# A hybrid decoder step: the next block's output projection before both halves of the last down part

## The chip, the cores and the metric

The kernel runs as one program on one core of one Trainium2 chip. The metric is the device time of an execution in microseconds (us); lower is better. The engines work side by side and wait for each other by semaphores: TensorE (PE, matmuls and transposes), VectorE (DVE), ScalarE (ACT), GpSimd (POOL), and SyncE (SP), which here issues nearly all DMAs in one fixed order.

## What is computed

One inference step of one decoder layer, for a prompt of 2048 tokens and a sample of 8 sequences of 8 tokens (64 rows). Cut to what matters here:

```
mix = concat(retention, stick_breaking_attention) @ w_out      # 1024 -> 1024
x   = x + g_m * mix
h   = rmsnorm(x, norm_ffn) * (1 + sc_f) + sh_f
a, bval = h @ w_up_gate, h @ w_up_val                           # 1024 -> 2816 each
conv = conv_b + sum_j a_ext[:, j:j+t] * conv_w[j]               # causal, width 3
ff  = (silu(conv) * bval) @ w_down                              # 2816 -> 1024
y   = rmsnorm(x + g_f * ff, norm_final)
```

Every matmul of these lines is done as three: each operand is split into a high and a low part of 32 bits each, and the products high x high, high x low and low x high are summed (`mm3`, lines 310 to 312).

## The kernel before, in words

The prompt is cut into four blocks of 512 tokens, each of four tiles of 128 tokens; the sample's 64 rows ride along with the last block as a fifth tile. After the input projections come two streams that are woven into one program: `attention([1, 2, 3])` and `mlps()` (line 1576). `mlps` does, block after block, the output projection with its residual and norm (`out_block`, line 1247) and the MLP (`ffn_block`, line 1327). Both are generators; `_weave` always steps the one that is behind by its share of planned work. The instructions that come out are then ordered on each engine by the framework's scheduler, so the order of the code is a guide and not the last word.

`ffn_block` goes over the 22 column tiles of the hidden layer in four parts of 6, 6, 6 and 4 (`PARTS`). A part does its up projections (features on the partitions, `act` is the moving operand), then its down projection in two halves of 512 output columns, each into four PSUM banks `d` (the sample's into a bank `z`), and adds them to the residual rows `x2` (`residual`, line 1321: DVE multiplies the bank by the gate `gp` into `hf`, then DVE or POOL adds `hf` to the rows `ff`). There are only four `d` banks, so a half can begin on a bank when `residual` of the half before has read it.

In the last part, the next block's `out_block` is run between the two halves (line 1422, `got = yield from after`). `out_block` loads two gates, the eight mixed-feature tiles `act<-mx` (512 KB each, into the same two `act` tiles that the up projection has just read), the four rows of `x`, and `w_out` in four loads of 1 MB (`raw`, two buffers). ACT and DVE split each `raw` in two pairs `whl` (three pairs fit). It returns a generator of features: normalised rows (`c`, `a`), PE transposes them (L416), ACT and DVE scale, shift and split them into `act` for the next up projection. In the second half, which goes tile by tile, one step of it is run after each tile; before the half, one step is run as well.

## Time and profile before

| | us |
|---|---|
| median of 3 runs | 3330.89 (3329.63 to 3334.44) |
| the profiled execution, its own time | 3337.49 |
| its span in the trace | 3335.8 |
| PE busy in the span | 3201.6 (96%) |
| DVE / ACT / POOL busy | 2086.6 / 1580.0 / 1023.7 |

The profiled execution is 6.6 us above the median. Matmuls are pipelined and their busy times overlap, so the pace of PE is read from one start to the next, and its idle time from the gaps that the timeline shows. The clock in a view is the granted clock of TensorE as a share of its full 2.4 GHz, averaged over the stretch; it has two levels, full and half.

### The profile page before, as it was taken

Reading aid. Unit: us, or ns where it says so; the run is one execution under the profiler, and the core shown is the slowest. Engines: PE = TensorE matmul, PEld = TensorE weight load, DVE = VectorE, ACT = ScalarE, POOL = GpSimd, SP = SyncE. Lnnn points to the kernel's source line nnn. Section 1 sums busy time; section 2 is a strip of 40 time slices with the busy share of each in tenths; the row PEclk is TensorE's granted clock in tenths of the full one; section 3 lists DMA queues with packets and bytes.
Section 4 is the critical chain, followed back from the end, with each engine's and each line's share of the span. In section 5 each row is a group of like instructions: output and inputs, shape, how many; then the busy total and the mean of one; then the engine's idle time right before and its main releaser. Section 6 shows DMA issues by size and latency. Waiting matters only on the chain. (4 is left out here: it accounts for less than half of the span.)

```text
span 3335.8 us, 50095 instructions
## 1 busy us (share of the span) xinstructions
PE 3201.6 (96%) x17879; PEld 2601.1 (78%) x17879; DVE 2086.6 (63%) x2989; ACT 1580.0 (47%) x2796; POOL 1023.7 (31%) x1841
## 2 busy tenths in 40 slices
PE   7999999999999889999999999999999999999998
PEld 5886777666887778878877778877788787799997
DVE  3245344245766587777778787787887873644445
ACT  3345335234444365555556455556555543533323
POOL 2012012013432343433444334344442432312113
PEclk8999999999999999999999999999999999999999
DMA  7757877885667843343454334354433335232221
GB/s 251 248 177 228 275 260 250 275 277 177 189 189 226 252 127 115 113 133 108 133 186 133 105 117 119 107 169 137 129 111 107 118 98 177 93 101 71 95 77 68
DMA packets 404247, 526.99 MB, mean 158 GB/s; under 512 B 25974, under 2 KB 242153, under 8 KB 403998
## 3 DMA queue, kind: packets, MB, share of 16 engines
q1 hardware_dynamic: 370078, 472.27, 45.3%
q10 hardware_dynamic: 33920, 51.52, 4.2%
q8 instruction: 142, 2.33, 0.3%
q14 instruction: 107, 0.88, 0.1%
HBM read 442.11 MB, written 81.60 MB: 157 GB/s over the span
## 5 line engine op out<-in xcount | busy, mean ns | idle before, releaser
L183 ACT CAST whl<-raw 128x1024 fp32r<-128x1024 f32 x408 | 427.5, 1049 | 1091.3 <-PE d L311 798.4
L165 DVE TENSOR_TENSOR whl<-raw,whl 128x1024 fp32r<-128x1024 f32 x408 | 517.8, 1270 | 577.0 <-ACT whl L183 568.8
L310 PE MATMUL d<-act,whl 128*128 128x512 f32 (+2 forms) x2016 | 745.0, 370 | 4.3 <-ACT whl L183 2.3
L312 PE MATMUL d<-act,whl 128*128 128x512 f32 (+2 forms) x2016 | 735.9, 365 | 1.2 <-DVE whl L165 1.2
L311 PE MATMUL d<-act,whl 128*128 128x512 f32 (+2 forms) x2016 | 733.7, 364 | 3.3 <-DVE act L165 2.4
L310 PEld LDWEIGHTS d<-act,whl 128*128 128x128 f32 x2016 | 384.8, 191 | 73.4 <-issue 11.1
L312 PEld LDWEIGHTS d<-act,whl 128*128 128x128 f32 x2016 | 383.9, 190 | 61.1 <-DVE whl L165 2.2
L311 PEld LDWEIGHTS d<-act,whl 128*128 128x128 f32 x2016 | 385.7, 191 | 58.7 <-DVE act L165 2.6
L310 PE MATMUL d<-whl,ff 128*128 128x512 f32 x704 | 279.3, 397 | 0.0
L311 PE MATMUL d<-whl,ff 128*128 128x512 f32 x704 | 278.8, 396 | 0.0
L312 PE MATMUL d<-whl,ff 128*128 128x512 f32 x704 | 278.1, 395 | 0.0
L310 PE MATMUL d<-whl,act 128*128 128x512 f32 x640 | 260.8, 409 | 10.3 <-ACT whl L183 9.2
L312 PE MATMUL d<-whl,act 128*128 128x512 f32 x640 | 258.5, 404 | 0.0
L311 PE MATMUL d<-whl,act 128*128 128x512 f32 x640 | 258.3, 404 | 0.0
L1172 DVE TENSOR_TENSOR_SCAN aom<-aom,acy 128x512 f32<-128x512 f32 x192 | 256.0, 1333 | 2.4 <-ACT aom L1158 1.7
L165 DVE TENSOR_TENSOR abe<-abe,aom 128x512 f32<-128x512 f32 (+2 forms) x320 | 229.7, 718 | 23.8 <-POOL abe L1162 2.3
L1196 PE MATMUL acc<-ahl,avv 128*128 128x512 f32 (+3 forms) x640 | 223.6, 410 | 15.2 <-DVE ahl L165 9.4
L1158 ACT ACTIVATE aom<-z,nb 128x512 f32<-128x512 f32 (+2 forms) x320 | 201.1, 628 | 61.2 <-PE z L1155 38.3
L1159 ACT ACTIVATE abe<-z,bb 128x512 f32<-128x512 f32 (+2 forms) x320 | 199.8, 624 | 0.0
L165 DVE TENSOR_TENSOR ahl<-z,ahl 128x512 fp32r<-128x512 f32 (+1 forms) x320 | 191.5, 598 | 10.7 <-ACT ahl L183 10.5
L1155 PE MATMUL z<-akk,aq 128*128 128x512 f32 (+3 forms) x640 | 190.5, 375 | 6.0 <-DVE ahl L165 3.1
L165 POOL TENSOR_TENSOR ff<-ff,hf 128x512 f32<-128x512 f32 (+1 forms) x101 | 161.0, 1624 | 90.2 <-DVE hf L165 76.2
(288 smaller groups left out, 5691.2 us busy)
## 6 DMA issues: line engine op xcount, KB each, us to landing
raw<-in_w_in SPq DMA_DIRECT2D x56, 1024.0 KB
raw<-in_w_up_gate SPq DMA_DIRECT2D x44, 1024.0 KB
raw<-in_w_up_val SPq DMA_DIRECT2D x44, 1024.0 KB
akk<-k SPq DMA_DIRECT2D x160, 256.0 KB
page<-in_cache_k_pages SPq DMA_DIRECT2D x128, 256.0 KB
vpage<-in_cache_v_pages SPq DMA_DIRECT2D x128, 256.0 KB
raw<-in_w_down SPq DMA_DIRECT2D x32, 1024.0 KB
raw<-in_w_ada SPq DMA_DIRECT2D x24, 1024.0 KB
```

The source lines that it names most:

```text
L165: eng.tensor_tensor(o, a, b, op)
L183: act.copy(hi, src)
L310: pe.matmul(ps, sh, mh, start=start, stop=False)
L311: pe.matmul(ps, sh, ml, start=False, stop=False)
L312: pe.matmul(ps, sl, mh, start=False, stop=stop)
L1155: pe.matmul(z[:, :n], qs[g, h][:, i * P : (i + 1) * P], kk[:, c, :n], start=c == 0, stop=c == 1)
L1158: act.activation(om[:, :n], z[:, :n], AF.Sigmoid, bias=nb[:, h : h + 1], scale=-SCALE)
L1159: act.activation(be[:, :n], z[:, :n], AF.Sigmoid, bias=bb[:, h : h + 1], scale=SCALE)
L1172: dve.tensor_tensor_scan(rv, rv, rv, init, ALU.mult, ALU.bypass)
L1196: pe.matmul(accs[0][:, cs], kv[u][1][:, kt, :], m[:, cs], start=(s == g and kt == 0 and c == 0), stop=(s == 0 and kt == NT - 1 and c == 1),)
```

## The change

The next block's `out_block` runs before both halves of the last down part. The steps of its features stand beside both halves: one after each of the two weight steps of half 0, then one after each tile of half 1; the step ahead of half 1 is gone. In `out_block`, `w_out`'s loads for the first half stand ahead of the gates and of the rows of `x`, which are loaded when the first half is at its middle (`rows`). The sample's tile goes first instead of last in the output projection and the features (`ordered`), its mixed features come in one load instead of eight, and short deferred jobs (`tick`) run in half 1 too.

```diff
--- before.py
+++ after.py
@@ -209,7 +209,7 @@
     mix_sc = [
         [T(dram, [P, 2, TB], F32, f"mx{g}{k}") for k in range(KT)] for g in range(NB)
     ]
-    mixs_sc = [T(dram, [P, 2, NS], F32, f"ms{k}") for k in range(KT)]
+    mixs_sc = T(dram, [KT, P, 2, NS], F32, "ms")
     gp_sc = [T(dram, [P, D], F32, f"gp{i}") for i in range(2)]
     gs_sc = [T(dram, [NS, D], F32, f"gs{i}") for i in range(2)]
 
@@ -361,7 +361,7 @@
     def by_tile(tiles, k0, n):
 
         order = [(k, tile) for k in range(k0, k0 + 2) for tile in tiles]
-        return sorted(order, key=lambda kt: kt[1]) if k0 == n - 2 else order
+        return sorted(order, key=lambda kt: tiles.index(kt[1])) if k0 == n - 2 else order
 
     def dense_pair(wts, acts, t, features=False):
 
@@ -1252,13 +1252,13 @@
         while ("attn", g) not in done or ("rdone", g) not in done:
             yield None
         xpool = xpools()
-        gates = [load_g(0, half, fp, samp and xpool) for half in range(2)]
+        ordered = tiles[NT:] + tiles[:NT]
         smp = T(xpool, [P, KT, 2, NS], F32R, "smp") if samp else None
         for k in range(KT):
             ld(acts[k // 4][:, k % 4, :, :TB], mix_sc[g][k])
-            if samp:
-                ld(smp[:, k], mixs_sc[k])
-        x2, ss = [], []
+        if samp:
+            ld(smp, mixs_sc.rearrange("k p c n -> p k c n"))
+        x2, ss, gates = [], [], []
 
         def squares(i, half):
             n = tiles[i][2]
@@ -1267,39 +1267,45 @@
                 junk[:n], x2[i][:n, half * 512 : half * 512 + 512], AF.Square, accum_out=ss[i][:n, half : half + 1]
             )
 
-        for i, o, n in tiles:
-            x = T(xpool, [P, 1024], F32, "ff")
-            ld(x[:n], xp[g * TB + o : g * TB + o + n, :] if i < NT else xs)
-            x2.append(x)
-            ss.append(T(small, [P, 2], F32, f"os{i}"))
+        def rows():
+            gates.append(load_g(0, 0, fp, samp and xpool))
+            for i, o, n in tiles:
+                x = T(xpool, [P, 1024], F32, "ff")
+                ld(x[:n], xp[g * TB + o : g * TB + o + n, :] if i < NT else xs)
+                x2.append(x)
+                ss.append(T(small, [P, 2], F32, f"os{i}"))
+            gates.append(load_g(0, 1, fp, samp and xpool))
+
         for half in range(2):
             pss = [pd() if i < NT else pz() for i, _, _ in tiles]
             for k0, (hi, lo) in w_tm(w_out, 0, KT, half * 512):
-                for k, tile in by_tile(tiles, k0, KT):
+                if half == 0 and k0 == 4:
+                    rows()
+                for k, tile in by_tile(ordered, k0, KT):
                     tok_mm(
                         pss[tile[0]], act_rows(k, tile, smp), (hi[:, k - k0, :], lo[:, k - k0, :]),
                         k == 0, k == KT - 1,
                     )
                 yield cost / 2
                 tick()
-            for i, o, n in tiles:
+            for i, o, n in ordered:
                 residual(pss[i], gates[half][i == NT], x2[i], half, n, fp, dve if half else pool)
                 if half == 0:
                     later.append([2, lambda i=i: squares(i, 0)])
         tick(9)
-        rs = []
-        for i, o, n in tiles:
+        rs = {}
+        for i, o, n in ordered:
             squares(i, 1)
-            rs.append(rows_rstd(ss[i], n))
+            rs[i] = rows_rstd(ss[i], n)
 
         def features():
             xn = {}
             for j in range(len(tiles) + 2):
                 if j >= 2:
-                    i, o, n = tiles[j - 2]
+                    i, o, n = ordered[j - 2]
                     to_features(xn[j - 2], o, n, coef[2], coef[3], acts, fp)
                 if j < len(tiles):
-                    i, o, n = tiles[j]
+                    i, o, n = ordered[j]
                     xa, xb = xn[j] = T(fp, [P, 512], F32, "c"), T(fp, [P, 512], F32, "a")
                     act.activation(xa[:n], x2[i][:n, :512], AF.Copy, scale=rs[i][:n, 0:1])
                     dve.tensor_scalar(xb[:n], x2[i][:n, 512:], rs[i][:n, 0:1], None, ALU.mult)
@@ -1330,7 +1336,7 @@
         tiles = TILES + ([(NT, TB, NS)] if samp else [])
         cost = 10.4 * t / 512
         gfs = [load_g(1, half, fp, samp and fp) for half in range(2)]
-        got, ss, ends = None, {}, []
+        got, feats, ss, ends = None, iter(()), {}, []
         ordered = tiles[NT:] + tiles[:NT]
 
         def gate(fi, outs):
@@ -1418,25 +1424,26 @@
                 sv(O["y_prompt"][g * TB + o : g * TB + o + n, :] if i < NT else O["y_sample"], y[:n, :D])
 
             for half in range(2):
-                if last and half and after is not None:
+                if last and not half and after is not None:
                     got = yield from after
+                    feats = got[1]
                 if last:
                     nf = T(fp, [P, 512], F32, "gp")
                     ld(nf, I["norm_final"][half * 512 : half * 512 + 512].partition_broadcast(P))
                 pss = [pd() if i < NT else pz() for i, _, _ in tiles]
                 if last and half:
-                    feats = got[1] if got else iter(())
-                    next(feats, None)
                     wts = list(w_tm(w_dn, f0, f1 - f0, half * 512))
                     for tile in ordered:
                         for q0, w in wts:
                             for q in range(2):
                                 one(pss, tile, f0 + q0 + q, w, q)
                         yield cost * (f1 - f0) / 4 / len(tiles)
+                        tick()
                         next(feats, None)
                     yield from feats
                     if after is not None:
                         first_gates[g + 1] = list(w_fm(w_ug, 0))
+                    tick(9)
                     for tile in ordered:
                         residual(pss[tile[0]], gfs[half][tile[0] == NT], x2[tile[0]], half, tile[2], fp, dve)
                         ends.append(finish(*tile, nf, pool if samp and tile[0] != NT - 1 else dve))
@@ -1449,6 +1456,8 @@
                         for q, tile in by_tile(tiles, q0, f1 - f0):
                             one(pss, tile, f0 + q, w, q - q0)
                         yield cost / 2
+                        if last:
+                            next(feats, None)
                     for i, o, n in tiles:
                         residual(pss[i], gfs[half][i == NT], x2[i], half, n, fp, dve if samp else pool)
                         if last:
```

What this does to the order on the engines at three places of the last block (the transition from block 2 to block 3), where attention has ended:

PE, where the last up projection ends (`d<-act,whl`). Before, half 0 of down follows (`d<-whl,ff`):

```order
L310 MATMUL d_30055<-act_115_194,whl_30051 128x512
L311 MATMUL d_30055<-act_115_194,whl_30051 128x512
L312 MATMUL d_30055<-act_115_194,whl_30052 128x512
L310 MATMUL d_30086<-whl_30092,ff_29849 128x512
L311 MATMUL d_30086<-whl_30093,ff_29849 128x512
L312 MATMUL d_30086<-whl_30092,ff_29849 128x512
```

With the change, the output projection of block 3 follows (`d<-whl,act`):

```order
L310 MATMUL d_30048<-act_108_187,whl_30044 128x512
L311 MATMUL d_30048<-act_108_187,whl_30044 128x512
L312 MATMUL d_30048<-act_108_187,whl_30045 128x512
L310 MATMUL d_30091<-whl_30098,act_107_186 128x512
L311 MATMUL d_30091<-whl_30099,act_107_186 128x512
L312 MATMUL d_30091<-whl_30098,act_107_186 128x512
```

The 48 matmuls of half 0 moved from between the two projections to behind the second one.

SP, the loads of the last block. Before, from the second gate (`gp`) to the second load of `w_out`; the first load of `w_out` stands far ahead of these rows:

```order
L171 DMA act_115_194<-mx_90_146 128x2x512
L171 DMA gp_30172<-gp_100_156 128x512
L171 DMA smp_30176<-ms_98_154 128x128
L171 DMA act_115_194<-mx_91_147 128x2x512
L171 DMA smp_30176<-ms_99_155 128x128
L171 DMA ff_30193<-in_x_prompt 128x1024
L171 DMA ff_30196<-in_x_prompt 128x1024
L171 DMA ff_30199<-in_x_prompt 128x1024
L171 DMA ff_30202<-in_x_prompt 128x1024
L171 DMA ff_30205<-in_x_sample 64x1024
L171 DMA raw_30291<-in_w_out 128x4x512
```

With the change, from the first load of `w_out` on:

```order
L171 DMA raw_30096<-in_w_out 128x4x512
L171 DMA raw_30162<-in_w_out 128x4x512
L171 DMA act_107_186<-mx_84_140 128x2x512
L171 DMA mx_91_147<-ahl_30038 128x512
L171 DMA act_107_186<-mx_85_141 128x2x512
L171 DMA mx_91_147<-ahl_30039 128x512
L171 DMA act_107_186<-mx_86_142 128x2x512
L171 DMA act_107_186<-mx_87_143 128x2x512
L171 DMA act_108_187<-mx_88_144 128x2x512
L171 DMA act_108_187<-mx_89_145 128x2x512
L171 DMA act_108_187<-mx_90_146 128x2x512
L171 DMA act_108_187<-mx_91_147 128x2x512
```

Both loads of `w_out` for the first half now stand ahead of the mixed features, and no gate is among them: the second gate's load (`gp`) moved far ahead, into block 2's first part. Behind these rows come `smp`, `gs`, the five rows of `x`, `gs`, and the third load of `w_out`.

DVE, the reading of half 0's banks (`hf<-d`, gate `gp`). Before, they stand between weight splits, ahead of the whole output projection:

```order
L165 TENSOR_TENSOR whl_30216<-raw_30213,whl_30215 128x1024
L165 TENSOR_TENSOR ff_30081<-c_29990,ff_30081 128x512
L165 TENSOR_TENSOR whl_30260<-raw_30213,whl_30259 128x1024
L165 TENSOR_TENSOR hf_30148<-d_30086,gp_25831 128x512
L165 TENSOR_TENSOR hf_30152<-d_30087,gp_25831 128x512
L165 TENSOR_TENSOR hf_30156<-d_30088,gp_25831 128x512
L165 TENSOR_TENSOR hf_30160<-d_30089,gp_25831 128x512
L165 TENSOR_TENSOR whl_30294<-raw_30291,whl_30293 128x1024
```

With the change, they stand in the middle of the features:

```order
L165 TENSOR_TENSOR hf_30567<-z_30562,coef_102_168 128x64
L165 TENSOR_TENSOR act_107_186<-hf_30551,act_107_186 128x4x64
L165 TENSOR_TENSOR hf_30567<-hf_30567,coef_103_169 128x64
L165 TENSOR_TENSOR hf_30567<-z_30562,coef_102_168 128x64
L1311 TENSOR_SCALAR a_30579<-ff_30175,rs_b_30455 128x512
L165 TENSOR_TENSOR hf_30567<-hf_30567,coef_103_169 128x64
L165 TENSOR_TENSOR hf_30582<-d_30476,gp_25824 128x512
L165 TENSOR_TENSOR act_108_187<-hf_30567,act_108_187 128x4x64
L165 TENSOR_TENSOR hf_30586<-d_30477,gp_25824 128x512
L165 TENSOR_TENSOR hf_30590<-d_30478,gp_25824 128x512
L165 TENSOR_TENSOR hf_30594<-d_30479,gp_25824 128x512
L1311 TENSOR_SCALAR a_30661<-ff_30178,rs_b_30463 128x512
```

The four readings moved behind the sample's features (`hf<-z`, 64 columns wide) and ahead of those of the other tiles.

## Rows read from the trace of the kernel before

**Rows 1.** The profile's page: busy us (share) of each engine; granted clock by 40 slices.

```profile
PE 3201.6 (96%) x17879; PEld 2601.1 (78%) x17879; DVE 2086.6 (63%) x2989; ACT 1580.0 (47%) x2796; POOL 1023.7 (31%) x1841
...
PEclk8999999999999999999999999999999999999999
```

**Rows 2.** Busy by stretch: us, PE, PEld, DVE, ACT, POOL (instructions), clock, DMA share, GB/s.

```profile
1740.00:1790.00 50.00, 41.12 (x240) 33.95 (x240) 42.53 (x62) 37.98 (x78) 26.49 (x52) 0.97 0.43 132
2310.00:2370.00 60.00, 50.38 (x275) 41.31 (x274) 54.80 (x74) 44.82 (x89) 34.98 (x55) 0.94 0.38 117
2400.00:2760.00 360.00, 359.52 (x1685) 288.01 (x1684) 280.22 (x334) 191.62 (x310) 131.39 (x217) 1.00 0.36 109
2795.00:2827.00 32.00, 27.55 (x119) 21.79 (x117) 7.28 (x10) 5.49 (x11) 10.07 (x8) 0.98 0.98 299
2820.00:2840.00 20.00, 14.21 (x52) 10.57 (x52) 5.37 (x5) 4.08 (x4) 0.00 (x0) 0.83 0.64 203
2880.00:2900.00 20.00, 13.91 (x74) 11.65 (x73) 16.45 (x38) 14.05 (x31) 6.97 (x7) 0.74 0.17 54
```

**Rows 3.** Waits of PE in 1740 to 1790 us: total us, times, longest us.

```profile
PE acc L1196 <- ACT ahl L183: 3.1, 2, 2.5
PE z L416 <- DVE hf L165: 1.4, 1, 1.4
```

**Rows 4.** Waits of PE in 2310 to 2370 us.

```profile
PE acc L1196 <- DVE ahl L165: 2.8, 2, 2.3
PE z L1184 <- ACT hf L428: 2.2, 1, 2.2
PE z L416 <- ACT hf L428: 1.8, 1, 1.8
```

**Rows 5.** Timeline of PE, last block: start, us, line, operation; idle before and its releaser.

```profile
2798.12 0.39 PE L310 MATMUL d<-whl,ff 128*128 128x512 f32 x1
...
2809.32 0.40 PE L310 MATMUL d<-whl,act 128*128 128x512 f32 x1
...
2828.30 1.22 PE L310 MATMUL d<-whl,act 128*128 128x512 f32 x2 [5.75 <-ACT whl L183]
...
2887.27 0.64 PE L416 MATMUL z<-con,c 64*128 64x64 f32 x4 [1.28 <-ACT hf L428]
...
2891.92 0.85 PE L310 MATMUL z<-act,whl 128*128 128x288 f32 x2 [3.40 <-ACT act L439]
```

**Rows 6.** Timeline of SP, last block: when loads are issued.

```profile
2782.56 0.37 SPq L171 DMA_DIRECT2D raw<-in_w_out  x1
2793.41 0.56 SPq L171 DMA_DIRECT2D act<-mx  x1
...
2810.31 0.32 SPq L171 DMA_DIRECT2D gp<-gp  x1
...
2812.42 1.95 SPq L171 DMA_DIRECT2D ff<-in_x_prompt  x4
...
2814.96 1.50 SPq L171 DMA_DIRECT2D raw<-in_w_out  x2
```

**Rows 7.** Timeline of ACT, last block.

```profile
2827.20 1.99 ACT L183 CAST whl<-raw 128x1024 fp32r<-128x1024 f32 x2 [13.46 <-DMA raw<-in_w_out]
```

**Rows 8.** Groups of instructions, 2500 to 3336 us: busy us, mean ns, idle before.

```profile
L165 DVE TENSOR_TENSOR hf<-d,gp 128x512 f32<-128x512 f32 x64 | 43.4, 684 | 6.9 <-PE d L312 4.8 <-POOL ff L165 1.3
...
L165 POOL TENSOR_TENSOR ff<-ff,hf 128x512 f32<-128x512 f32 (+1 forms) x25 | 38.4, 1567 | 50.0 <-DVE hf L165 50.0
```

**Rows 9.** Timeline of DVE, last block: first and last of the sample's features.

```profile
2889.67 0.35 DVE L165 TENSOR_TENSOR hf<-z,coef 128x64 f32<-128x64 f32 x2 [1.16 <-POOL act L165]
...
2893.41 0.35 DVE L165 TENSOR_TENSOR hf<-hf,coef 128x64 f32<-128x64 f32 x2
```

**Rows 10.** Timeline of DVE in the features of block 2.

```profile
2327.54 0.68 DVE L165 TENSOR_TENSOR act<-hf,act 128x512 fp32r<-128x512 f32 x1
2328.14 1.78 DVE L165 TENSOR_TENSOR hf<-hf,coef 128x512 f32<-128x512 f32 x1
```

**Rows 11.** Timeline of POOL in the same stretch.

```profile
2327.82 1.55 POOL L165 TENSOR_TENSOR act<-hf,act 128x512 fp32r<-128x512 f32 x1 [1.14 <-ACT act L439]
```

**Rows 12.** Timeline of PE, first block, start of its second half.

```profile
1153.47 0.50 PE L310 MATMUL d<-whl,act 128*128 128x512 f32 x1 [0.99 <-DVE hf L165]
```

**Rows 13.** Timeline of SP, first block.

```profile
1144.03 1.89 SPq L171 DMA_DIRECT2D ff<-in_x_prompt  x4
1145.97 1.68 SPq L171 DMA_DIRECT2D aq<-q  x2
1147.69 2.10 SPq L171 DMA_DIRECT2D akk<-k  x2
```

## The prediction

> **What bounds the kernel now.** I read the page first: PE is busy 96% of the span, DVE 63%, ACT less [rows 1]. PE is therefore the engine whose idle time counts, and only 4% of it is there to be had. The table by stretch says where it lies. In 360 us of plain up and down projections woven with attention, PE is busy 359.52 us at full clock, with DVE at 280 of 360, or 78% [rows 2]. Nothing can be gained there. The losses of the MLP stage stand at the transitions from one block to the next, which is what the change touches. PE's idle time there is 50 - 41.1 = 8.9 us (block 0 to 1), 60 - 50.4 = 9.6 us (1 to 2), and for the last block 20 - 14.2 = 5.8 us in its output projection and 20 - 13.9 = 6.1 us in its features [rows 2]: 30.4 us in all. The granted clock is also below 1 there: 0.97, 0.94, 0.83 and 0.74, a shortfall of 1.5, 3.6, 3.4 and 5.2 us. Part of that shortfall falls into the idle time and costs nothing twice; I count half of it, 0.8, 1.8, 1.7 and 2.6 us, with none and all of it as the bounds. So 37 us are lost at the places of the change, at most 44.
>
> Then the waits. In blocks 1 and 2 PE waits for ACT and DVE: transposes (L416) for features, attention matmuls for their evictions [rows 3, 4]. In the last block, where attention has ended, the timeline shows two other things [rows 5]. The output projection stops for 5.75 us at its second half of weights. Later the first up projection stops for 3.40 us because its features are not ready. The SP timeline tells why the weights were late: the second `w_out` load is issued only at 2814.96, behind the gate `gp` (2810.31) and the rows of x (2812.42), and ACT gets it at 2827.20 [rows 6, 7].
>
> **The change part by part.** The matmuls, splits, transposes and bytes are the same before and after; the eight loads of `smp` become one, which is SP's time and hidden. The edit in `by_tile` and the `tick` calls reorder short jobs off PE's path; I cost them at nothing, as PE has other matmuls queued while they run. If that cover fails it shows in the bank wait that I price below.
>
> *Weights of the output projection, last block.* Both loads of the first half now stand ahead of the mixed features, so the 5.8 us and their clock part of 1.7 go: -7.5. What is late next is the third load, for the second half. Ahead of it, from the first mixed-feature load on, stand 4.2 MB of these, 0.5 MB of stores, 0.5 of `smp`, 0.3 of `gs` and 2.4 of x, and it is 1.0 MB itself: 8.9 MB. At the 299 GB/s that the queue moves in this stretch [rows 2] that takes 29.8 us, counted from 2795, so it lands at 2824.8. The output projection would start at 2798.12, where half 0 starts now, and its first half is 112 matmuls; 48 of them take 11.20 us (2798.12 to 2809.32) [rows 5], so it ends at 2824.2. With ACT's split PE waits some 1.6 to 3 us. I take 2.5; none if SP issues more tightly, 5 with a fall of the clock. Sum -5.
>
> *Features, last block.* Before, half 1 with 48 matmuls (11.2 us) covers the chain from the last residual to the features; now 96 do (22.4 us). The 6.1 us and their clock part of 2.6 go: -8.7. A new wait comes in their place: DVE reads half 0's banks behind the sample's features. These take 2889.67 to 2893.76, 4.1 us [rows 9], and start only when PE has transposed them behind half 0; each reading takes 0.68 us [rows 8]. PE meanwhile has four more groups of transposes, about 1.8 us, then needs the first bank: 4.1 + 0.7 - 1.8 = 3 us, and I take 3.3 with the wait for the z banks. The last features, behind all this on DVE, may be 1 us late, and the clock 0.4. Sum -4, between -8.7 (no bank wait) and 0.
>
> *Blocks 1 and 2.* The same cover of 11.2 us is added, but here attention loads DVE. In block 2's stretch DVE has 54.8 us of work to PE's 50.4 [rows 2], so 4.4 us of the idle time is DVE's throughput and 5.2 is latency. The moved half brings 11.2 us of PE work at the plain stretch's DVE share of 78%, 8.7 us, so the surplus falls from 4.4 to 1.9: -2.5. Of the latency and of the clock part I take half, as the chain still starts at the same residual: -2.6 and -0.9. In block 1 the surplus of 42.5 - 41.1 = 1.4 goes, with half of 7.5 and of 0.8: -5.5. Sum -11.5, between -5 (latency stays) and -21 (all goes). Against it stand two new waits per block. The bank wait is 3.3 us at most and 0 at least; between the halves more attention stands here as cover, so I take 1. The mixed features lose the 11.2 us of half 0 as their cover, and the output projection needs the first right after the last up matmul. The nearest row is the last block's: the first load is issued at 2793.41, 4.7 us before that point [rows 5, 6], because it waits only for the part of `act` that it overwrites. At 299 GB/s its 0.5 MB take 1.8 us, and each next load 1.8 us against the 2.8 us that PE needs per feature tile (12 matmuls). I take 0.5 us, between none and the 9 us of the rival below. So +3, sum -8.5.
>
> *Block 0.* Its features are not spread, but its loads move: attention's loads now stand ahead of gate and x. Their issue takes 1.68 and 2.10 us [rows 13], so x comes up to some 4 us later, and PE already waits 0.99 us for the residual there [rows 12]. Attention's first matmuls move ahead with them and fill a part: +1, between 0 and 4.
>
> **The sum**: -5 - 4 - 8.5 + 1 = -16.5 us, or 3321.0 against the profiled execution's 3337.49. That execution is 6.6 us above the median, which I take off: **3314.4**.
>
> **The rivals.** *DVE and POOL get in each other's way.* The moved half puts four POOL additions of 1.57 us [rows 8] into each feature stretch, where DVE is over 90% busy. In block 2 a DVE operation that takes 0.68 us elsewhere took 1.78 while POOL ran one of 1.55 us [rows 10, 11]. If each added POOL operation stretches one DVE operation by 1.1 us, that is 4.4 us in each of blocks 1 and 2: -16.5 + 8.8 = -7.7, or 3323.2. Against it: only some operations beside POOL show this, and DVE's four readings keep their 0.68 on average while POOL adds behind them [rows 8]. The Trainium skill (Perfetto Trace Analysis, Optimizing Scalar/DVE Operations) says that GpSimd and DVE share a read port of SBUF, so that work given to one may not relieve the other. By that rule this case would be the likely one; the trace agrees in rows 10 and 11 alone.
>
> *The gain is eaten by the new waits.* Bank waits of 3.3 us in blocks 1 and 2 (+4.6 over what I took), the third weight load at 5 (+2.5), x of block 0 at 4 (+3) and no latency gained (+7.6): -16.5 + 17.7 = +1.2, or 3332. For it: PE's own order puts half 1's first tile right behind the transposes. Against it: all four would have to stand at their bad ends.
>
> *The output projection starts without its features, and the kernel is slower.* If the loads were held until the whole last up projection has read `act`, half of the mixed features, four loads, would have to land first: 7 us and some 2 us from issue on, 9 us per block, 27 in all, -16.5 + 1 + 27 = +11.5, or 3342. It decides from a wait of about 6 us per block on. Against it is the issue at 2793.41 in the middle of the last up matmuls, and ACT's and SP's rows show no such hold now.
>
> **How the numbers follow.** About 0.2% (6.7 us) is what a measurement of this kernel can tell from no change. The forecast, between 3304 and 3320, gets 0.63; the shared port 0.17, most of it still faster than 3324.2; the eaten gain 0.12; the slower case 0.08. So faster 0.77, same 0.15, slower 0.08. The range runs from 3300 (bank wait and third load at nothing, most of the latency gone) to 3329 (the eaten gain's better half).
>
> **What would show it.** In the trace after: no wait of several us on ACT's split in the middle of the last output projection, at most 3 us between its halves; a wait of PE for `hf<-d` or z between the halves of the last down part, some 3 us in the last block; the first up matmuls of a block starting within 1 us of the last transposes; idle time in blocks 1 and 2 about half, with DVE still full. I would be wrong if PE waited for `act<-mx` at the start of an output projection, if DVE operations beside POOL's additions grew beyond 1 us, or if the stretches of blocks 1 and 2 lost as much as before.

## The result and the profile after

The changed kernel is slower: 3342.06 us against 3335.65 us, medians of 17 runs each. One run of the change, at a granted clock of 0.573, took 4993.88 us and is left out of the ratio, which is 1.0025 with a 95% interval from 1.0014 to 1.0036, or +8 us (the medians alone differ by 6.4). Forecast was -16.5 us, or 3314.4, counted from a median of three runs that is 4.8 us below the one of 17. The profiled execution of the changed kernel took 3350.06 us, span 3348.4. Its page:

```profile
PE 3203.3 (96%) x17879; PEld 2600.5 (78%) x17879; DVE 2093.4 (63%) x2989; ACT 1578.9 (47%) x2796; POOL 1020.6 (30%) x1841
```

The instructions of PE and DVE are as many as before [rows 1], yet DVE is 6.8 us longer busy. As all kernels here run the same 17879 matmuls, the start of PE's n-th matmul in one trace can be set against the n-th in another; the difference grows only where time is lost or won. It changes at five places, and is flat between them (0.4 us at most for the changed kernel; e1, e6 and e8 lose 3.6, 3.2 and 1.6 us between the first place and the second). The first place is around block 0's output projection (matmuls 6500 to 7500), then the transitions from block 0 to 1 (9600 to 10200) and 1 to 2 (12200 to 12900), then the last block's projection (14700 to 15020) and its features (15020 to 15240). All of it, for every kernel of this study, against the execution of before, in us:

| kernel | block 0 | 0 to 1 | 1 to 2 | last projection | last features | measured ratio [95%] |
|---|---|---|---|---|---|---|
| the change | +5.7 | +4.5 | +0.6 | -4.1 | +3.2 | 1.0025 [1.0014, 1.0036] |
| e1 no move | +3.3 | 0.0 | +1.2 | -8.0 | +1.7 | 1.0000 [0.9989, 1.0011] |
| e2 rows early in block 0 | +0.8 | +5.9 | +0.7 | -4.5 | +3.1 | 1.0010 [0.9999, 1.0022] |
| e3 additions on DVE | +5.3 | +5.2 | +2.1 | -2.5 | +2.2 | 1.0040 [1.0026, 1.0054] |
| e4 squares late | +2.7 | +8.0 | +4.8 | -3.6 | +1.6 | 1.0044 [1.0029, 1.0060] |
| e5 features earlier | +3.9 | +7.2 | +4.5 | -3.8 | -1.3 | 1.0025 [1.0013, 1.0038] |
| e6 e1 with rows early | +1.2 | +1.3 | +1.3 | -8.0 | +1.8 | 0.9998 [0.9987, 1.0009] |
| e7 no closing work | +4.3 | +0.2 | -4.5 | -2.4 | -1.3 | 0.9988 [0.9978, 0.9998] |
| e8 e5 with rows early | +3.3 | +6.2 | +4.6 | -3.7 | -1.3 | 1.0022 [1.0010, 1.0033] |
| e9 no squares | +3.3 | +7.7 | +2.0 | -4.3 | +4.9 | 1.0024 [1.0010, 1.0037] |
| e10 no multiplications | +7.4 | +4.1 | -1.6 | -4.2 | +0.9 | 0.9998 [0.9987, 1.0008] |
| e11 no additions | +3.5 | +4.7 | -2.0 | -4.2 | +0.5 | 0.9998 [0.9988, 1.0008] |
| e12 last weights only | +3.8 | -1.1 | -0.1 | -8.2 | +0.6 | 0.9964 [0.9951, 0.9978] |
| e13 e12, rows late in block 0 | +6.3 | +0.1 | +0.1 | -8.2 | +0.6 | 0.9992 [0.9980, 1.0003] |
| e14 e12 again | +2.9 | +0.1 | -0.1 | -8.2 | +0.6 | 0.9977 [0.9965, 0.9988] |

How far chance goes shows in equal code: 0 to 1 in e12, e13 and e14, which is there the code of before, reads as before within 1.1 us; the last two columns repeat within 0.1 (e12 to e14). Block 0 is uneven (+2.9 and +3.8 in e14 and e12, whose block 0 is that of before), and ahead of it executions of any kernel differ by -9.0 to +2.6 us; that part is left out of the table.

Busy by the three feature stretches (0 to 1, 1 to 2, last features; columns as in rows 2), before:

```profile
1689.40:1816.70 127.30, 117.92 (x602) 95.62 (x601) 103.06 (x137) 80.60 (x149) 55.68 (x104) 0.99 0.46 140
2245.50:2396.60 151.10, 141.43 (x701) 113.87 (x700) 124.43 (x156) 92.86 (x173) 73.76 (x105) 0.98 0.47 144
2865.00:2910.00 45.00, 38.91 (x222) 33.78 (x221) 34.87 (x66) 28.45 (x64) 15.94 (x33) 0.89 0.24 83
```

and after:

```profile
1697.50:1829.40 131.90, 119.64 (x602) 97.19 (x601) 108.73 (x139) 82.80 (x157) 65.01 (x106) 0.97 0.44 135
2258.60:2410.30 151.70, 141.18 (x701) 114.00 (x700) 125.67 (x156) 92.92 (x173) 69.67 (x104) 0.98 0.46 141
2874.50:2922.70 48.20, 37.80 (x222) 32.76 (x221) 36.28 (x62) 29.93 (x64) 26.49 (x34) 0.96 0.25 84
```

The first two stretches hold the projection and half 0 in both kernels, the last one holds the features: there POOL has 26.49 - 15.94 = 10.6 us more for the same matmuls. The clock is better there (0.96 for 0.89), but PE stands still for longer (48.2 - 37.8 = 10.4 us for 6.1). The timeline of PE in it and in the projection ahead of it:

```profile
2826.32 0.47 PE L319 MATMUL z<-whl,smp 128*128 128x512 f32 x1 [0.75 <-DMA smp<-ms]
2841.28 0.50 PE L319 MATMUL z<-whl,smp 128*128 128x512 f32 x1 [2.12 <-ACT whl L183]
...
2883.86 0.50 PE L310 MATMUL d<-whl,ff 128*128 128x512 f32 x1 [0.41 <-DVE hf L165]
...
2892.31 0.63 PE L416 MATMUL z<-con,a 128*128 128x128 f32 x4 [2.59 <-DVE hf L165]
...
2905.52 0.61 PE L310 MATMUL d<-act,whl 128*128 128x288 f32 x1 [5.24 <-DVE hf L165]
```

The 5.75 us of [rows 5] are gone and 2.12 (plus 0.75 for `smp`) stand for them. But a transpose waits 2.59, and the first up matmul 5.24 instead of 3.40. DVE and ACT tell why:

```profile
2891.47 1.45 DVE L165 TENSOR_TENSOR hf<-z,coef 128x512 f32<-128x512 f32 x2 [2.39 <-POOL ff L165]
2892.84 3.33 DVE L165 TENSOR_TENSOR hf<-hf,coef 128x512 f32<-128x512 f32 x2
```

```profile
2886.59 0.63 ACT L1413 ACTIVATE hf<-ff 128x512 f32<-128x512 f32 x1 [2.94 <-POOL ff L165]
...
2891.47 0.63 ACT L1413 ACTIVATE hf<-ff 128x512 f32<-128x512 f32 x1 [2.10 <-POOL ff L165]
```

DVE waits for a buffer of `hf` (there are three), which POOL's addition still holds; two operations that take 0.68 us each elsewhere then take 3.33 together; ACT waits in the squares of half 0 (L1413) for POOL. In block 2 POOL works through one piece:

```profile
2329.95 3.79 POOL L165 TENSOR_TENSOR ff<-ff,hf 128x512 f32<-128x512 f32 x3
2333.71 2.19 POOL L165 TENSOR_TENSOR ff<-ff,gp 128x512 f32<-128x512 f32 x1
2335.86 1.44 POOL L165 TENSOR_TENSOR ff<-ff,hf 128x512 f32<-128x512 f32 x1
...
2337.85 4.64 POOL L165 TENSOR_TENSOR ff<-ff,gp 128x512 f32<-128x512 f32 x3
```

These are half 0's four additions and four multiplications by the norm's gain (`first_half`), 3.79 + 2.19 + 1.44 + 4.64 = 12.1 us, in the middle of the features. DVE beside them:

```profile
2332.48 2.35 DVE L1172 TENSOR_TENSOR_SCAN aom<-aom,acy 128x512 f32<-128x512 f32 x1
2334.75 1.43 DVE L1311 TENSOR_SCALAR a<-ff,rs_b 128x512 f32<-128x512 f32 x1
2336.10 1.75 DVE L165 TENSOR_TENSOR abe<-abe,aom 128x512 f32<-128x512 f32 x1
2337.77 0.68 DVE L165 TENSOR_TENSOR hf<-z,coef 128x512 f32<-128x512 f32 x1
```

In the kernel before, the same eight operations stand at the start of the output projection, whose matmuls begin at 2249.92 us, ahead of the features:

```profile
2246.61 6.40 POOL L165 TENSOR_TENSOR ff<-ff,hf 128x512 f32<-128x512 f32 x4 [0.41 <-DVE hf L165]
2254.30 7.38 POOL L165 TENSOR_TENSOR ff<-ff,gp 128x512 f32<-128x512 f32 x4
```

### The profile page after: what moved, and what is told of

It is laid out like the page before. It is cut to its first block, busy times and chain, and to the rows that moved or that the text cites. A ratio compares the mean times of both kernels' runs of the same rounds, so it can differ in the third digit from the quotient of the medians.

```text
span 3348.4 us, 50078 instructions
## 1 busy us (share of the span) xinstructions
PE 3203.3 (96%) x17879; PEld 2600.5 (78%) x17879; DVE 2093.4 (63%) x2989; ACT 1578.9 (47%) x2796; POOL 1020.6 (30%) x1841
## 4 chain that ended last, share of the span: by engine, by line
PE 45%; DVE 2%; POOL 2%; ACT 1%; issue 1%; DMA 0%; POOLq 0%; SPq 0%; DVEq 0%; ACTq 0%
PE d L310 11%; PE d L312 11%; PE d L311 11%; PE acc L1196 3%; PE z L1155 2%; PE z L1184 2%; PE z L312 1%; PE z L310 1%; PE z L311 1%; POOL ff L165 1%; DVE whl L165 1%; DVE hf L165 0%; PE z L320 0%; PE z L319 0%; POOL rs_b L165 0%
## 5 line engine op out<-in xcount | busy, mean ns | idle before, releaser
L310 PE MATMUL d<-act,whl 128*128 128x512 f32 (+2 forms) x2016 | 743.8, 369 | 13.7 <-DVE hf L165 10.0
L310 PEld LDWEIGHTS d<-act,whl 128*128 128x128 f32 x2016 | 383.9, 190 | 82.8 <-issue 13.5
L310 PE MATMUL d<-whl,ff 128*128 128x512 f32 x704 | 280.6, 399 | 1.9 <-DVE hf L165 1.9
L310 PE MATMUL d<-whl,act 128*128 128x512 f32 x640 | 261.3, 410 | 8.7 <-ACT whl L183 5.3
L1360 DVE SCALAR_TENSOR_TENSOR c<-a,vecs,c 128x512 f32<-128x512 f32 x176 | 135.0, 767 | 81.6 <-ACT c L1357 46.8
```

Source lines behind the costliest of these rows:

```text
L310: pe.matmul(ps, sh, mh, start=start, stop=False)
L1360: dve.scalar_tensor_tensor(c[:, :TB], a[:, j : j + TB], cw(j), c[:, :TB], ALU.mult, ALU.add)
```

## The experiments

### Is it the move? (e1, e6)

e1 is the changed kernel with the move undone (its new `tick` calls go, too); e6 also has block 0's rows early.

```diff
-                if last and not half and after is not None:
+                if last and half and after is not None:
                     got = yield from after
-                    feats = got[1]
...
+                    feats = got[1] if got else iter(())
+                    next(feats, None)
...
-                        if last:
-                            next(feats, None)
```

> The output projection as the change has it (its loads, the sample's tile first), but run between the two halves of the last down part, with the features beside the second half alone, as before the change. The two traces, matmul by matmul, put the change's loss at +5.7 us in block 0, +4.5 in block 0 to 1, +1.0 in block 1 to 2, and -1.0 in the last block (-4.1 in the projection, +3.1 in the features). Theory A (the move brings half 0's closing work, its additions on POOL and its squares on ACT, in among the features): blocks 1 and 2 come back to the kernel before, 0 within 1.5 us each, the last block's features to 0, its projection keeps -4 or better, block 0 keeps +5.7; about +1.5 us in all, ratio 1.0005. Rival B (the edits inside the output projection cost the time, the move doesn't): blocks 1 and 2 keep +4.5 and +1.0, ratio 1.002 or more.

> The output projection's edits without the move (as in the first run), and with block 0's gates and rows ahead of its weights (as in the second). If the parts add up by their places: block 0 +0.8 instead of +3 to +7, blocks 1 and 2 +0 and +1.2, the last block's projection -8.0 and its features +1.7, so -4.3 us to the kernel before, ratio 0.9987. If block 0's difference is chance between executions, the ratio stays at the 1.000 of the first run.

Measured: 1.0000 and 0.9998. In the total, B's 1.002 is out and A's 1.0005 is near: by the ratios the move costs 8.3 us (the change against e1) or 4.0 (e2 against e6). The places say less. The projection gains 8.0 us without the move, more than the 4.1 with it, and the last features lose 1.7 and 1.8 instead of 3.2. But 1 to 2 (+1.2, +1.3) is no better than with the move, and the 0.0 and +1.3 in the column 0 to 1 flatter: e1 and e6 lose another 3.6 and 3.2 us in the 50 matmuls right ahead of that column, at one wait of attention (e6, waits of PE in 1685 to 1710 us):

```profile
PE acc L1196 <- DVE ahl L165: 2.7, 1, 2.7
```

With it, 0 to 1 costs 3.6 and 4.5 us, as much as with the move. The wait comes from the edits inside the projection, as rival B has it: in e1, two splits of weights stand ahead of attention's `ahl` on DVE, beside half 0's multiplications on POOL, and take 4.50 us where one takes 1.22 elsewhere; before, no split stood there, and `ahl` began at 1687.08.

```profile
1686.61 4.50 DVE L165 TENSOR_TENSOR whl<-raw,whl 128x1024 fp32r<-128x1024 f32 x2
1691.04 0.68 DVE L165 TENSOR_TENSOR ahl<-z,ahl 128x512 fp32r<-128x512 f32 x1
```

So e6's -4.3 us by places were not reached; I had counted only the places of the change. That the move costs time at the transitions is left to the experiments below.

### Block 0's rows (e2, e13, e14)

e2 is the change with `rows()` called ahead of the weights' loop in block 0.

```diff
+        if g == 0:
+            rows()
         for half in range(2):
...
-                if half == 0 and k0 == 4:
+                if half == 0 and k0 == 4 and g > 0:
```

> The change, with block 0's gates and rows of x loaded ahead of its first weights' matmuls, as before the change; the other blocks as changed. Theory C (attention's loads ahead of x and the gate made block 0's residual late, and its 5.7 us): block 0 returns to within 1.5 us of the kernel before, all else as in the change: -5 us against the change, ratio 1.001 to the kernel before. Rival D (block 0's loss is a difference between two profiled executions, as the +2.5 us are that stand ahead of it): no change in the ratio, 1.0025.

Measured 1.0010, block 0 at +0.8. Since block 0 is uneven from execution to execution, e13 and e14 repeated it on a kernel with nothing else changed there (e12, below):

> The kernel with the last block's weights first (nothing moved), and in block 0, too, the gates and rows of x loaded at the middle of the output projection's first half. Theory C (late rows make block 0's residual late): 2 to 5 us slower than the same kernel with block 0's rows early, which runs beside it, and PE waits for DVE's hf in block 0's second half for 2 us or more. Rival D (the differences in block 0 are chance between executions): the two kernels' medians agree within 1.5 us, whatever the single profiled executions show.

Measured: 3330.71 us with late rows, 3326.96 with early ones on the same chip; 3.75 us by the medians, +6.3 - 2.9 = 3.4 by the places. Waits of PE in e13 (1155 to 1210 us):

```profile
PE z L416 <- ACT c L1314: 4.0, 2, 2.3
PE d L310 <- DVE hf L165: 3.2, 3, 1.5
```

and in e14 (1148 to 1200 us):

```profile
PE z L416 <- ACT c L1314: 3.3, 2, 1.7
PE z L1184 <- DVE abe L165: 2.9, 3, 1.7
...
PE d L310 <- DVE hf L165: 0.8, 1, 0.8
```

e14 has a wait of attention (L1184, 2.9 us) that e13 has not, so these two lists alone don't settle it. But the gaps ahead of L310 tell the two kinds apart in every kernel: in block 0 (matmuls 6500 to 7500, gaps over 0.2 us) they come to 3.6 to 4.7 us in the ten kernels with late rows and to 1.4 to 1.7 us in the six with early ones, the kernel before among these. DVE's readings need the gate. SP issues it in e13 behind attention's loads, 3.9 us behind the last mixed feature (1145.59 to 1149.48); in e14 it is next (1140.53 to 1141.18):

```profile
1145.59 0.61 SPq L171 DMA_DIRECT2D act<-mx  x1
1146.30 1.19 SPq L171 DMA_DIRECT2D aq<-q  x2
1147.54 1.25 SPq L171 DMA_DIRECT2D akk<-k  x2
1148.84 0.59 SPq L171 DMA_DIRECT2D avv<-v  x1
1149.48 0.50 SPq L171 DMA_DIRECT2D gp<-gp  x1
```

```profile
1140.53 0.61 SPq L171 DMA_DIRECT2D act<-mx  x1
1141.18 1.07 SPq L171 DMA_DIRECT2D gp<-gp  x2
```

Theory C holds in its cause, with 1.9 to 3.3 us of waiting. What it is worth in the total is less certain: by the ratios of the four pairs that differ in block 0's rows, 5.0 us (the change and e2), 0.7 (e1, e6), 1.0 (e5, e8) and 5.0 (e13, e14). The rest of the +5.7 is within what block 0 shows for equal code.

### Moving the closing work elsewhere (e3, e4)

e3 adds on DVE; e4 puts the squares and multiplications off until behind the features.

```diff
-  residual(pss[i], gfs[half][i == NT], x2[i], half, n, fp, dve if samp else pool)
+  residual(pss[i], gfs[half][i == NT], x2[i], half, n, fp, dve if samp or last else pool)
```

```diff
-  later.append([1, lambda i=i, n=n, nf=nf: first_half(i, n, nf)])
+  later.append([6, lambda i=i, n=n, nf=nf: first_half(i, n, nf)])
```

> The change, with half 0's additions of the last down part on DVE (0.69 us each) instead of POOL (1.57 us). Theory A1 (POOL's additions hold the buffers of hf and, through the squares, ACT's queue): the wait of DVE's hf on POOL's ff, 2.4 us in the last block, goes, the 2.6 us before the transposes and most of the 5.2 us before the first up matmul go: -5 us in the last block; in blocks 1 and 2, where DVE gets 2.8 us more work, -1 each: ratio 1.0005. Rival A2 (DVE's work is the limit of the features): the last block gains at most 1 us, blocks 1 and 2 lose 2 each: ratio 1.0035.

> The change, with half 0's squares (ACT) and multiplications by the norm's gain (POOL) put off until the features are issued. Theory A3 (ACT waits 5.4 to 5.8 us per block for POOL's additions in these squares, and the features' evictions and casts stand behind them): the waits of ACT's squares on POOL leave the features' stretch, PE's 2.6 to 2.9 us before the second transposes go in each block, and the first up matmul starts 2 us earlier or more: -3 us per block, ratio 0.9998. Rival A1 (the buffers of hf that POOL's additions hold are the wait): DVE's 2.4 us on POOL's ff stays and with it the loss: ratio 1.002.

Measured: 1.0040 and 1.0044, neither faster than the change (1.0014 to 1.0036, which both intervals overlap), so neither of my mechanisms is the whole of it. In e3 DVE no longer waits for POOL in the last features, which gain 1.0 us, but ACT's squares now wait for DVE as long as they did for POOL (two waits, 5.2 us, in 2876 to 2923):

```profile
ACT hf L1413 <- DVE ff L165: 5.2, 2, 3.0
```

while 0 to 1 and 1 to 2, where DVE is loaded, lose 0.7 and 1.5. In e4 the waits went on to other instructions of ACT (1691 to 1827):

```profile
ACT hf L1266 <- POOL ff L165: 5.0, 1, 5.0
ACT hf L428 <- POOL ff L165: 3.9, 1, 3.9
```

### Starting the features earlier (e5, e8)

```diff
                     got = yield from after
                     feats = got[1]
+                    next(feats, None)
```

> The change, with one more step of the features ahead of half 0, so that the first tile's transposes (in the last block the sample's) stand in the middle of half 0 instead of behind it. Theory F (the features start too late: in the last block PE could transpose from about 2874, when the scaled rows are there, but does so only at 2879.5, behind all 48 matmuls of half 0): the stretch of features ends one tile, 2.8 to 5.6 us, earlier, and the wait before the first up matmul (1.9, 2.9 and 5.2 us in blocks 1, 2 and 3) goes: -2 to -4 us per transition, ratio 1.000. Rival A (half 0's closing work on POOL and ACT stands behind the same number of features as before and takes its time wherever these begin): the waits move to a later tile, less than 1.5 us gained per transition, ratio 1.002.

> Both repairs on the whole change: one step of the features ahead of half 0, and block 0's gates and rows ahead of its weights. If both theories hold (late rows, 5 us; late features, 2 to 4 us per transition) they add: ratio 0.998 to 0.999, faster than both kernels. If the closing work sets the transitions instead, only block 0's 5 us come back: ratio 1.0005 to 1.001, as in the second run.

Measured: 1.0025 and 1.0022. Theory F holds where attention has ended: the last features go from +3.2 to -1.3, 4.5 us, and the 5.24 us before the first up matmul fall to nothing, though one transpose still waits 3.69. In 0 to 1 and 1 to 2 it costs 2.7 and 3.9 us instead. There, as I read it, the features take the place of attention's work; PE waits for both in e5, 0 to 1:

```profile
1755.73 1.11 PE L416 MATMUL z<-con,a 128*128 128x128 f32 x4 [2.66 <-DVE hf L165]
...
1787.25 0.80 PE L1196 MATMUL acc<-ahl,avv 128*128 128x512 f32 x1 [6.30 <-ACT ahl L183]
```

e8's two repairs therefore don't make it faster than before.

### Leaving the closing work out (e7, e9, e10, e11)

```diff
-  residual(pss[i], gfs[half][i == NT], x2[i], half, n, fp, dve if samp else pool)
+  residual(pss[i], gfs[half][i == NT], x2[i], half, n, fp, dve if samp else pool) if not (last and after is not None) else tt(dve, T(fp, [P, 512], F32, "hf")[:n], fold(pss[i], n, fp)[:n], gfs[half][i == NT][:n, :], ALU.mult)
...
-  later.append([1, lambda i=i, n=n, nf=nf: first_half(i, n, nf)])
+  if after is None:
+      later.append([1, lambda i=i, n=n, nf=nf: first_half(i, n, nf)])
+  else:
+      pool.memset(ss[i], 1.0)
```

That is e7; e9 leaves out the squares alone (four short memsets stand for them), e10 the multiplications alone, e11 the additions alone.

> The change without half 0's closing work of the last down part in blocks 0 to 2: DVE still reads the four banks, but the four additions on POOL, the four squares on ACT and the four multiplications by the norm's gain on POOL are left out (so the first half of the output's columns is not what it should be). Theory A (this work, 12.5 us of POOL in one piece, stands among the features and costs the time): POOL is idle there, DVE's operations beside it fall back to 0.68 us, and the transitions fall from +4.5, +0.6 and +3.2 to -2 to -4 each: ratio 0.9985 or less. Rival F (the features start behind half 0 and only half 1 covers them, whatever else is there): the transitions keep their +4.5, +0.6 and +3.2 within 1 us, ratio 1.002.

> The change with only half 0's squares of the last down part left out in blocks 0 to 2 (the scale of the output's rows is not what it should be); the additions and multiplications on POOL stay. With all three left out the three transitions (0 to 1, 1 to 2, last features) went from +4.5, +0.6, +3.2 to +0.2, -4.5, -1.3 against the kernel before, 14.3 us. Theory A3 (the squares hold ACT's queue while they wait for POOL's additions, 5.4 to 5.8 us per block, and the features' evictions stand behind them): at least 7 of the 14.3 us come back, ratio 1.0005 or less. Rival A1 (POOL's eight operations stretch DVE's beside them and hold the hf buffers, whatever ACT does): at most 4 us come back, ratio 1.0015 or more.

> The change with only half 0's multiplications by the norm's gain on POOL left out in blocks 0 to 2 (the first half of the output's columns lacks the gain); nothing waits for these in the stretch. Theory A1 (POOL's time beside DVE): half of POOL's operations go, and with them 5 to 8 of the 14.3 us, ratio 1.0005 to 1.001. Theory A3 (ACT's queue behind the squares, which wait for the additions): the multiplications stand between the additions on POOL (after the third) but cost only the last of the squares, so 2 us at most per block, 1 to 4 us in all: ratio 1.0015.

> The change with only half 0's additions on POOL left out in blocks 0 to 2 (DVE reads the banks, but the residual rows lack half 0); squares and multiplications stay. The buffers of hf come free at once, and the squares no longer wait for POOL. Theory A3, and the rival that the hf buffers are the wait: 9 us or more of the 14.3 come back, ratio 1.000 or less. Theory A1 (POOL's time beside DVE, half of which stays): 5 to 8 us, ratio 1.0005 to 1.001.

Measured: e7 0.9988, 0.12% below before, and 13.9 us below the change at the three feature places (+8.3 to -5.6). Without the closing work the move brings 5.6 us at these places; the forecast had 8.5 + 4 = 12.5. Its stretches:

```profile
1687.00:1814.50 127.50, 117.43 (x602) 95.72 (x601) 103.27 (x138) 80.02 (x150) 50.75 (x102) 0.99 0.45 140
2243.70:2390.30 146.60, 139.44 (x702) 112.84 (x701) 121.91 (x156) 90.55 (x165) 56.73 (x100) 0.99 0.48 148
2856.20:2899.90 43.70, 37.99 (x222) 32.58 (x221) 32.47 (x61) 27.04 (x56) 13.90 (x25) 0.96 0.27 93
```

DVE has lost no operation (2989 in all; 355 for 357 fall into these stretches) and is busy 103.27 + 121.91 + 32.47 = 257.7 us for 270.7, 13.0 us less. By groups, with the change (2326 to 2350 us; mean ns behind the busy time):

```profile
L1172 DVE TENSOR_TENSOR_SCAN aom<-aom,acy 128x512 f32<-128x512 f32 x2 | 4.1, 2048 | 0.0
...
L165 DVE TENSOR_TENSOR abe<-abe,aom 128x512 f32<-128x512 f32 x3 | 3.1, 1034 | 0.0
L165 DVE TENSOR_TENSOR hf<-z,coef 128x512 f32<-128x512 f32 x4 | 2.7, 674 | 0.0
```

and in e7 (2310 to 2336 us):

```profile
L1172 DVE TENSOR_TENSOR_SCAN aom<-aom,acy 128x512 f32<-128x512 f32 x3 | 3.8, 1267 | 0.0
...
L165 DVE TENSOR_TENSOR abe<-abe,aom 128x512 f32<-128x512 f32 x4 | 2.7, 674 | 0.0
L165 DVE TENSOR_TENSOR hf<-z,coef 128x512 f32<-128x512 f32 x4 | 2.7, 666 | 0.0
```

These two windows don't hold quite the same operations. The whole trace of the change shows more: two kinds of DVE operation of one size, 224 of each, the first with both operands in SBUF, the second with its first operand in a PSUM bank.

```profile
L165 DVE TENSOR_TENSOR abe<-abe,aom 128x512 f32<-128x512 f32 x224 | 186.7, 833 | 17.5 <-POOL abe L1162 1.8
L165 DVE TENSOR_TENSOR ahl<-z,ahl 128x512 fp32r<-128x512 f32 x224 | 151.7, 677 | 12.0 <-ACT ahl L183 12.0
```

Of the first, those that run beside a POOL operation for a fifth of their time or more take 1.00 us on the mean and 1.75 at most, the others 0.69; of the second none takes over 0.69, beside POOL or not.

e10 and e11 each take about half of POOL's eight operations away; both measure 0.9998, where e9, which takes nothing of POOL's time, measures 1.0024 on the same chip, as the change does. That is 8.7 us, clear of the intervals. So POOL's eight operations are what costs, each half of them enough to matter, and ACT's wait in the squares is a symptom of them: A1, not A3. By the places it is less even: e10 and e11 bring 5 us of the 13.9 each (to +3.4 and +3.2 in sum), all of it in 1 to 2 and the last features, while 0 to 1 keeps its loss (+4.1 and +4.7) until all eight are gone (e7, +0.2). e9 is worse at the places than the change by 6 us (+14.6 in sum); that is not explained, its total does not show it, and it says how far the places of one execution can be trusted. e11 frees the `hf` buffers at once and brings 5 us instead of the 9 or more that were expected if they were the wait, so they are not all of the cost. How the rest divides between DVE's stretching and the wait for these buffers was not separated: more buffers were not tried.

### What is worth keeping (e12, e14)

The kernel before, with the load order of the last block alone:

```diff
-        gates = [load_g(0, half, fp, samp and xpool) for half in range(2)]
+        gates = [] if samp else [load_g(0, half, fp, samp and xpool) for half in range(2)]
...
+        if not samp:
+            rows()
         for half in range(2):
             pss = [pd() if i < NT else pz() for i, _, _ in tiles]
             for k0, (hi, lo) in w_tm(w_out, 0, KT, half * 512):
+                if samp and half == 0 and k0 == 4:
+                    rows()
```

> The kernel before, with one thing of the change: in the last block the output weights of the first half are loaded ahead of the gates and the rows of x, which are loaded at the middle of the first half. Nothing is moved in blocks 0 to 2. If the gain of 8 us in the last projection (PE's 5.75 us wait on ACT's split and the clock behind it) stands by itself: -6 to -8 us in all, ratio 0.9976 to 0.9982, faster than both kernels. If it was bought with the other edits' losses, or if the third load is late instead: -3 us or less, ratio 0.999 or more.

> The kernel before with the last block's weights first, again, on the same chip as the run beside it. By the places alone it should be some 8 us faster than the kernel before, ratio 0.9976; the first time it measured 0.9964. If that was luck of the chip, 0.9976 or above; if it holds, 0.997 or less.

Measured 0.9964 [0.9951, 0.9978] and 0.9977 [0.9965, 0.9988]: 12.0 and 7.7 us below before, and faster than the change. By the places, the last projection alone gives 8.2 us. PE has no gap left there (e12, with the kernel before behind it):

```profile
2776.40:2851.00 74.60, 74.60 (x322) 59.45 (x321) 28.75 (x33) 23.76 (x40) 23.33 (x21) 1.00 0.62 197
```

```profile
2782.20:2865.00 82.80, 77.01 (x322) 60.59 (x321) 28.06 (x33) 24.12 (x40) 20.65 (x21) 0.96 0.56 178
```

e1 and e6 load the last weights early, too, and win 8.0 us there, yet their totals are even. So, without the move, the other edits inside the projection cost about as much as the last weights bring. The wait for `ahl` shown above is one part of it (3.2 to 3.6 us); the others were not tried one by one.

## Why the prediction was wrong

**The failed step is the one that cost nothing.** "The edit in `by_tile` and the `tick` calls reorder short jobs off PE's path; I cost them at nothing." These jobs are half 0's squares and multiplications, and with its additions they are the closing work that came with the moved half. I let the half bring 11.2 us of PE work and 8.7 us of DVE work, and left POOL's 12.1 us per transition out of the sum; the rival of the shared port has the additions alone, about half of it. Before, the output projection covered this; now it stands among the features. The cover that I named, PE's queue, ran out: in the last features PE stands still for 10.4 us, and its two longest waits are for DVE, which is slower beside POOL. Leaving POOL's and ACT's closing work out takes the ratio from 1.0025 to 0.9988, 12.3 us, half of the 25 us between forecast and result. Of the other half, 12.5 - 5.6 = 6.9 us are gain from the longer cover that did not come even then. Term by term:

**Blocks 1 and 2**, forecast -8.5: measured +5.1 in the change, +6.6 in e2. Without the closing work -4.3 (e7), half of the forecast even then, and all of it in 1 to 2; why the longer cover gives no more was not tested.

**Last features**, forecast -4: measured +3.2; -1.3 in e7. The wait for the banks, priced at 3.3 us, is 0.41 (the row at 2883.86). The later start (behind all of half 0, e5) and POOL (e7) took 4.5 us each when removed one at a time; removing either is enough to reach -1.3, and neither reaches -4.

**Last weights**, forecast -5: measured -4.1 (-2.4 to -4.5 in all kernels with the move), right in the main, with the late third load at 2.12 us for the 2.5 that I took. I missed that the same loads without the move give -8.2 (e12): then half 0 stands ahead of the projection, and its loads have that much longer.

**Block 0**, forecast +1 with 4 as its bound: 1.9 to 3.3 us more waiting, within the bound.

**The rivals.** Two of the prediction's three signs of being wrong came: DVE operations beside POOL grew beyond 1 us, and blocks 1 and 2 lost as much as before. The shared port was the right mechanism with the wrong count: four POOL operations in two places at 1.1 us, 8.8 us, where there are eight in three places, 13.9 us by the places and 12.3 by the ratios. Even so it forecast a faster kernel, as it kept the other gains. The runs show which operations pay: `abe`, with both operands in SBUF, goes from 674 to 1034 ns and the scans from 1267 to 2048, while `hf<-z`, whose first operand is a PSUM bank, keeps its 674. The Trainium skill (SBUF — State Buffer, SBUF: two separate sides) says that DVE's second pair of ports is shared with GpSimd as an exclusive lock, held for a whole instruction, which DVE needs for two SBUF inputs; by that rule `hf<-z` would go free, and the trace agrees. The slower rival had the right sign and the wrong cause: in the three feature stretches PE waits nowhere for `act<-mx`. That its 3342 is the measured median is luck, and its sum has a slip: the 1 us already counted for this wait comes off, so -16.5 - 1 + 27 = +9.5. The eaten gain, at +1.2, was wrong in its terms: the bank waits of 3.3 us that it puts into blocks 1 and 2 are 0.7 each, and the third load's 5 is 2.12.

## What to carry to other kernels

Work that is moved as a cover for something else brings its own closing work on the other engines. Before it counts as cover, list every instruction that follows from it, deferred jobs too, and ask which engine runs them beside what. A gain that needs one load to be earlier is best taken by that load alone: here that was the only kernel with no work left out that became faster.

## What was not expected of the hardware

Leaving out 24 operations of POOL and 12 of ACT per execution (e7) took 13.0 us from DVE's busy time in the three stretches, though none of its own instructions went (e9, without the squares alone, took 4.0, so not all of it need be POOL's), so the busy time of an engine is no measure of its own work where another one reads beside it. And moving the four additions per block from POOL to DVE (e3) brought nothing: DVE's busy time rose from 108.7 + 125.7 + 36.3 = 270.7 us to 274.2, with nine more operations in the stretches.
